# A two-layer diffusion backbone on one core: the pins of the norm seams, the order of the first loads, and the neighbourhood bias laid out by diagonals on the host

## The chip, the cores and the metric

The kernel runs as one program on one core of one Trainium2 chip. The metric is the device time of one execution in microseconds (us), as the median of several runs. Engines are named as in the profile: PE is TensorE (PEld its weight loads), DVE is VectorE, ACT is ScalarE, POOL is GpSimd, SP is SyncE, from whose queue nearly all transfers are issued.

## The reference, cut to what matters

Two streams of 256 tokens, the latent x and the context z, go through two layers of width 1024. With `mx` and `mz` the nine shift, scale and gate vectors that a matrix `w_mod` gives for a layer:

```
for l in range(2):
    x = x + 0.5 * mx[2] * swiglu(modulate(rms_norm(x), mx[0], mx[1]), w1, w3, w2)       # ffn1, and z likewise
    hx = modulate(rms_norm(x), mx[3], mx[4]) @ w_in                                     # and hz likewise
    mix_x, mix_z = token_mixing(hx, hz, ...)   # Fourier | neighbourhood attention | gated linear attention | GQA
    x = x + mx[5] * (mix_x @ w_out)                                                     # and z, in layer 0 only
    x = x + 0.5 * mx[8] * swiglu(modulate(rms_norm(x), mx[6], mx[7]), v1, v3, v2)       # ffn2, z in layer 0 only
# neighbourhood attention of a latent token: a window of 4 rows by 16 columns, and all context tokens
s_win = q . k_window * scale + rpb[head, row offset + 7, column offset + 15]
s_ctx = q . k_ctx * scale
```

The table `na_rpb` has 15 x 31 values for each of 4 heads and 2 layers.

## The kernel before, in words

Every product of activations and weights is done as three matmuls of reduced precision: weights are split into `whi` and `wlo`, activations into `hh` and `hl`, and hi·hi, lo·hi and hi·lo are summed. The activations lie as eight tiles X[d] of 128 channels by 512 tokens; stream s=0 is the latent half of a tile, s=1 the context half.

Weights come in the order in which they are used. SP loads a piece to one of three buffers `raw`; `w_conv` turns it into `whi` on ACT (L248) and `wlo` on DVE (L251), four buffers of each. `w_fill` converts until `lead` pieces lie ready. The order of instructions on each engine is set by a scheduler when the program is built; `issue_after(i)` keeps an instruction behind i, `after_products(n, fn)` calls fn once n more triples of products have been written, and `high_priority` moves instructions ahead.

Between two of the four parts of a layer lies a *norm seam*. The last part's output is added to X[d] by DVE (L479 of the ffn), ACT squares it (L308), DVE adds the last square to `ss` (L311), PE sums `ss` over the channels (`pb`, L323, from `norm_stat`), DVE makes `ms` (L331), POOL the power `rs` (L333), PE spreads it over the partitions (`pb<-cst,rs`, L340, from `norm_bcast`), and `norm_apply` makes for each d `htmp` (DVE L360), `hh` (ACT L362) and `hl`: on DVE (L367) for even d, on ACT and POOL (L364, L365) for odd d. PE does stream 0 first and begins the next part's products on it while stream 1 goes through this chain. `LAGS` says how many triples of products PE puts ahead of `pb` and ahead of the spreading, for each stream; `AHEAD` how many weight conversions are put in after the norm of stream 0 and how far the lead reaches at the end of a part; `HLD` which `hl` a conversion's `wlo` is put behind.

In the mixing, `bias_load` (L855) brings the neighbourhood bias of a head into one slot (two rows) of `biases` as four strips of 64 partitions, each of 64 x 4 runs of 256 B; in layer 0 three slots serve four heads, so that head 3 is loaded when slot 0 has been read for the last time (L760). `bias_mask` (L867, POOL) subtracts it from the window's mask. `ke` (L658 to L661, POOL) and `pa` (L672, PE) are steps of the gated linear attention, `rs` of L540 the power of a per-head norm (`rms_tok`), `nt` (L544, DVE) its result.

At the start the first eight columns of modulations are made by 32 loads of `w_mod` (`wfirst`, L137) and `modps` matmuls (L144), four groups q of two channel tiles each, while the first weight pieces and X are loaded.

## Time and profile before

| | |
|---|---|
| median of 3 runs | 1748.44 us (1746.54 to 1750.69) |
| the profiled execution | 1751.36 us |
| its span, first to last instruction | 1749.6 us |
| mean granted clock of TensorE | 0.990 of full speed |
| busy: PE / PEld / DVE / ACT / POOL | 1696.8 / 1478.8 / 1104.0 / 667.2 / 215.7 us |
| PE idle over the span | 1749.6 - 1696.8 = 52.8 us |

The span is the profiled execution's work; the 1.8 us between it and that execution's time lie ahead of the first and behind the last instruction. A clock of 0.990 is a mean over the span: for short stretches it is half. Busy time of PE holds matmuls that run at the half clock, so what the clock costs does not show as idle time.

### The profile page before, as it was taken

Reading aid. Unit: us, or ns where it says so; the run is one execution under the profiler, and the core shown is the slowest. Engines: PE = TensorE matmul, PEld = TensorE weight load, DVE = VectorE, ACT = ScalarE, POOL = GpSimd, SP = SyncE. Lnnn points to the kernel's source line nnn. Section 1 sums busy time; section 2 is a strip of 40 time slices with the busy share of each in tenths; the row PEclk is TensorE's granted clock in tenths of the full one; section 3 lists DMA queues with packets and bytes.
Section 4 is the critical chain, followed back from the end, with each engine's and each line's share of the span. In section 5 each row is a group of like instructions: output and inputs, shape, how many; then the busy total and the mean of one; then the engine's idle time right before and its main releaser. Section 6 shows DMA issues by size and latency. Waiting matters only on the chain.

```text
span 1749.6 us, 28022 instructions
## 1 busy us (share of the span) xinstructions
PE 1696.8 (97%) x11174; PEld 1478.8 (85%) x11174; DVE 1104.0 (63%) x1834; ACT 667.2 (38%) x1124; POOL 215.7 (12%) x252
## 2 busy tenths in 40 slices
PE   6999999998989999999999999999999899989999
...
PEclk9999999999989999999999999999999999999999
...
GB/s 331 186 192 161 216 204 193 109 100 114 76 54 47 25 157 176 199 165 182 109 96 72 97 199 223 169 196 225 180 79 90 98 121 80 53 122 198 182 194 137
DMA packets 92274, 254.03 MB, mean 145 GB/s; under 512 B 17648, under 2 KB 28144, under 8 KB 91760
## 3 DMA queue, kind: packets, MB, share of 16 engines
...
HBM read 251.16 MB, written 1.05 MB: 144 GB/s over the span
## 4 chain that ended last, share of the span: by engine, by line
PE 87%; DVE 4%; DMA 3%; ACT 2%; issue 1%; POOL 1%; SPq 1%; POOLq 0%; ACTq 0%
PE p L284 48%; PE py L284 23%; PE pt L284 6%; PE pyo L284 3%; DVE wlo L251 1%; DMA biases<-in_na_rpb_dram 1%; PE po L788 1%; PE prT L779 1%; PE sc L756 1%; ACT whi L248 1%; PE pf L284 1%; PE pa L672 1%; SPq L860 0%; DMA raw<-in_f1w_dram 0%; DMA wfirst<-in_wmodf_dram 0%
## 5 line engine op out<-in xcount | busy, mean ns | idle before, releaser
L248 ACT CAST whi<-raw 128x1024 fp32r<-128x1024 f32 (+2 forms) x356 | 339.3, 955 | 858.2 <-PE p L284 277.8
L251 DVE TENSOR_TENSOR wlo<-raw,whi 128x1024 fp32r<-128x1024 f32 (+2 forms) x356 | 397.8, 1120 | 219.3 <-ACT whi L248 212.4
L284 PE MATMUL p<-hl,whi 128*128 128x512 f32 (+1 forms) x1504 | 525.5, 351 | 2.0 <-DVE hl L367 1.4
L284 PE MATMUL p<-hh,wlo 128*128 128x512 f32 (+1 forms) x1504 | 525.2, 350 | 0.3 <-DVE wlo L251 0.3
L284 PE MATMUL p<-hh,whi 128*128 128x512 f32 (+1 forms) x1504 | 523.0, 351 | 1.8 <-ACT hh L362 1.1
L284 PEld LDWEIGHTS p<-hl,whi 128*128 128x128 f32 x1504 | 283.4, 189 | 40.5 <-DVE hl L367 1.9
L284 PEld LDWEIGHTS p<-hh,wlo 128*128 128x128 f32 x1504 | 283.3, 189 | 38.5 <-DVE wlo L251 0.6
L284 PEld LDWEIGHTS p<-hh,whi 128*128 128x128 f32 x1504 | 281.5, 189 | 40.5 <-ACT hh L362 2.0
L169 DVE CUSTOM_DVE_ANT_0 mprod<-wmod,crow 128x1024 f32<-128x1024 f32 x256 | 302.2, 1221 | 0.0
L284 PE MATMUL py<-gh,wlo 128*128 128x512 f32 (+1 forms) x764 | 265.0, 347 | 0.0
L284 PE MATMUL py<-gl,whi 128*128 128x512 f32 (+1 forms) x764 | 264.8, 347 | 0.0
L284 PE MATMUL py<-gh,whi 128*128 128x512 f32 (+1 forms) x764 | 264.3, 348 | 0.0
L311 POOL TENSOR_TENSOR ss<-ss,sq 128x512 f32<-128x512 f32 (+1 forms) x34 | 40.9, 1202 | 1045.4 <-ACT sq L308 1044.0
L409 DVE TENSOR_TENSOR g<-p,sl 128x512 f32<-128x512 f32 (+1 forms) x88 | 55.0, 625 | 179.4 <-PE p L284 178.9
L284 PEld LDWEIGHTS py<-gl,whi 128*128 128x128 f32 x764 | 143.9, 188 | 18.4
L284 PEld LDWEIGHTS py<-gh,wlo 128*128 128x128 f32 x764 | 143.8, 188 | 18.3
L284 PEld LDWEIGHTS py<-gh,whi 128*128 128x128 f32 x764 | 143.6, 188 | 18.2
L284 PE MATMUL pt<-whi,hl 128*128 128x256 f32 x448 | 133.0, 297 | 7.3 <-POOL hl L365 7.2
L284 PE MATMUL pt<-whi,hh 128*128 128x256 f32 x448 | 133.4, 298 | 1.5 <-ACT nt L533 1.3
L284 PE MATMUL pt<-wlo,hh 128*128 128x256 f32 x448 | 131.1, 293 | 0.0
L479 DVE SCALAR_TENSOR_TENSOR X<-py,mod,X 128x256 f32<-128x256 f32 x112 | 50.3, 481 | 96.5 <-PE py L284 96.4
L284 PEld LDWEIGHTS pt<-whi,hl 128*128 128x128 f32 x448 | 89.0, 199 | 9.7 <-POOL hl L365 9.2
...
## 6 DMA issues: line engine op xcount, KB each, us to landing
wmod<-in_wmodt_dram SPq DMA_DIRECT2D x128, 512.0 KB, 3.9
...
raw<-in_f1w_dram SPq DMA_DIRECT2D x32, 320.0 KB, 2.9
raw<-in_f2w_dram SPq DMA_DIRECT2D x32, 320.0 KB, 2.9
...
```

What stands on the lines that cost most here:

```text
L169: nc.vector.tensor_tensor_reduce(out=prod, in0=raw, in1=crow[:, s], scale=1.0, scalar=0.0, op0=ALU.mult, op1=ALU.add, accum_out=acc[:, s, ...
L248: nc.scalar.copy(hi[:, :k * n], raw[:, :k * n])
L251: wlo[0] = nc.vector.tensor_tensor(out=lo[:, :k * n], in0=raw[:, :k * n], in1=hi[:, :k * n].bitcast(F32), op=ALU.subtract).ins
L284: nc.tensor.matmul(ps, w, x, start=first and i == 0, stop=last and i == len(parts) - 1)
L311: (nc.vector if d == KD - 1 else eng).tensor_tensor(out=st["ss"][:, c], in0=st["ss"][:, c], in1=sq[:, c], op=ALU.add)
L409: nc.vector.tensor_tensor(out=g[:, :n], in0=p3[:, :n], in1=sl[:, :n], op=ALU.mult)
L479: nc.vector.scalar_tensor_tensor(out=X[mt][:, c], in0=py[:, c], scalar=mcol(l, m, mt, s), in1=X[mt][:, c], op0=ALU.mult, op1=ALU.add)
L672: nc.tensor.matmul(pa[w * b:w * b + w, c * w:c * w + w], ke[hs, k0:k0 + w], qe[hs, q0:q0 + w], start=True, stop=True)
L756: nc.tensor.matmul(ps[:, :n], q[:, e, (t % 2) * P:(t % 2 + 1) * P], ks[e][:, T - n:T], start=i == 0, stop=i == 1)
L779: nc.tensor.transpose(pt[:, c * P:(c + 1) * P], pr[e][:, (2 * half + i) * P:(2 * half + i + 1) * P], ident)
L788: last_mm = nc.tensor.matmul(po[64 * e:64 * e + 64, c0:c0 + P], vs[e][4 - nkt + kt], prT[:, (2 * e + i) * P:(2 * e + i + 1) * P], start=kt ...
```

## The change

1. Pins of the seams. `LAGS` for stream 1 goes from 6 to 12 triples (into the mixing) and 14 (into an ffn). A conversion put in at a seam has both its halves, `whi` and `wlo`, put behind the end of a stream's `norm_apply` (`st["end", s]`); before, `wlo` alone was put behind one `hl`. An ffn's first pieces are filled to three more behind the end of stream 0. The last square and addition of a norm get high priority.
2. `mm3` does hi·hi, lo·hi (`wlo`), hi·lo (`hl`), with the last two swapped.
3. First loads. All of X goes first, then a weight piece, the eight `wfirst` of group 0, a weight piece, the eight of group 1, two weight pieces, the last sixteen. `w_mod`'s first part is laid out on the host so that each `wfirst` is one run of 2 KB a partition (before: two of 1 KB).
4. Bias. The host lays `na_rpb` out by diagonals (`nab`), so that a load is one contiguous piece a partition: 768 KB for slots 0 to 2 in layer 0 and 256 KB for head 3, 1 MB in layer 1. The load stands behind the queries' unit; clearing and masking stand behind the last `rms_tok` power so far.

```diff
-LAGS = {3: ((6, 6), (4, 4)), 6: ((6, 6), (4, 4)), 0: ((6, 6), (4, 4))}
+LAGS = {3: ((6, 12), (4, 4)), 6: ((6, 14), (4, 4)), 0: ((6, 14), (4, 4))}
-AHEAD = {3: (1, 1), 6: (0, 2), 0: (0, 2)}
+AHEAD = {3: (1, 2), 6: (0, 2), 0: (0, 2)}
-HLD = (2, 6)
+HLD = (6, 6)
...
-            v = a["wmodf"][k * P:(k + 1) * P, 256 * q:256 * q + 256]
-            nc.sync.dma_start(out=raw.rearrange("p (m c) -> p m c", m=2),
-                              in_=bass.AP(tensor=v.tensor, offset=v.offset, ap=[list(v.ap[0]), [D, 2], list(v.ap[1])]))
+            nc.sync.dma_start(out=raw, in_=a["wmodf"][q, k])
...
-        nc.scalar.copy(hi[:, :k * n], raw[:, :k * n])
+        with tc.issue_after(after[0]) if after is not None else nullcontext():
+            nc.scalar.copy(hi[:, :k * n], raw[:, :k * n])
         lo = tp.tile([P, 1024], F32R, tag="wlo", name="wlo", bufs=nb)
-        with tc.issue_after(after) if after is not None else nullcontext():
+        with tc.issue_after(after[1]) if after is not None else nullcontext():
...
-        product(((wh[:, k, :], xh), (wh[:, k, :], xl), (wl[:, k, :], xh)), ps, first, last)
+        product(((wh[:, k, :], xh), (wl[:, k, :], xh), (wh[:, k, :], xl)), ps, first, last)
...
+        if d1 == KD:
+            st["end", s] = (last, st["hl", s, KD - 2][1])
...
                 for i in range(AHEAD[m][0] if n > S else 0):
-                    w_conv(after=st["hl", 0, HLD[0]])
+                    w_conv(after=st["end", 0])
             elif AHEAD[m][0]:
-                w_fill(after=st["hl", 1, HLD[1]])
+                w_fill(after=st["end", 1])
...
+                if ("end", 0) in st and start is None:
+                    lead[0] = LEAD + 1
+                    w_fill(after=st["end", 0])
+                    lead[0] = LEAD
...
-        def bias_load(heads):
-            rp = a["na_rpb"]
-            for hd in heads:
-                for r in range(4):
-                    o = rp.offset + ((l * 4 + hd) * 15 + 7 - r) * 31 - 48
-                    nc.sync.dma_start(
-                        out=biases[(r % 2) * 64:(r % 2) * 64 + 64, 2 * (hd % slots) + r // 2].rearrange("p (a b) -> p a b", a=4),
-                        in_=bass.AP(tensor=rp.tensor, offset=o, ap=[[1, 64], [31, 4], [1, 64]]))
+        def bias_load(h0, h1):
+            i = h0 % slots
+            nc.sync.dma_start(out=biases[:, 2 * i:2 * (i + h1 - h0)], in_=a["nab"][l][:, 2 * h0:2 * h1])
...
         def bias_ready():
-            nc.gpsimd.memset(biases[:, 2 * slots], 0.0)
-            bias_mask(range(slots))
+            with tc.issue_after(pw[0]):
+                nc.gpsimd.memset(biases[:, 2 * slots], 0.0)
+                bias_mask(range(slots))
...
-                        bias_load((3,))
+                        bias_load(3, 4)
...
-            "G": (gla_in,), "R": (gla_r,), "N": (bias_in, lambda: na_qk(nqT, pairs_q, V_NAQ), lambda: na_qk(nkS, pairs_all, V_NAK), na_v, bias_ready),
+            "G": (gla_in,), "R": (gla_r,), "N": (lambda: na_qk(nqT, pairs_q, V_NAQ), bias_in, lambda: na_qk(nkS, pairs_all, V_NAK), na_v, bias_ready),
...
                 for d in range(KD):
-                    if d % 2 == 0:
-                        load_x(d)
-                        load_x(d + 1)
-                        next(ld)
-                        mods_product(ps0, d // 2, first[0][-1])
+                    load_x(d)
                     norm_square(st, npool, d, 0, 2, nc.vector)
+                w_conv()
...
+def _diagonals(rpb):
+    import numpy as np
+
+    p = np.arange(P)[:, None, None]
+    key = np.arange(256)[None, None, :]
+    at = (7 - 2 * np.arange(2)[None, :, None] - p // 64 + key // 64) * 31 + p % 64 + key % 64 - 48
+    flat = rpb.reshape(-1)
+    head = 15 * 31 * np.arange(8)[:, None, None, None]
+    return flat[np.clip(head + at, 0, flat.size - 1)].reshape(2, 4, P, 2, 256).transpose(0, 2, 1, 3, 4).reshape(2, P, 8, 256)
```

How the instructions then stand is shown at three places. The first is the seam of layer 0 from ffn1 into the mixing. On DVE before, where stream 0's `htmp` and `hl` are being made (X_89 is the last tile of stream 1 to be added; what stands in brackets are the engines and queues whose semaphores the instruction waits for):

```order
L360 SCALAR_TENSOR_TENSOR htmp<-X_86,mod_97,pb 128x256 [waits DVE_49]
L367 SCALAR_TENSOR_TENSOR hl_3256<-htmp,mod_97,hh_3255 128x256 [waits Activation_49]
L479 SCALAR_TENSOR_TENSOR X_89<-py,mod_97,X_89 128x256 [waits PE_49]
L251 TENSOR_TENSOR wlo<-raw,whi 128x1024 [waits DMAHW4_49]
L251 TENSOR_TENSOR wlo<-raw,whi 128x1024 [waits DMAHW5_49]
L360 SCALAR_TENSOR_TENSOR htmp<-X_87,mod_97,pb 128x256 [waits DVE_49]
L360 SCALAR_TENSOR_TENSOR htmp<-X_88,mod_97,pb 128x256 [waits Pool_49]
L367 SCALAR_TENSOR_TENSOR hl_3269<-htmp,mod_97,hh_3268 128x256 [waits Activation_49]
L311 TENSOR_TENSOR ss<-ss,sq 128x256 [waits Activation_49]
```

On DVE after the change, at the same place:

```order
L485 SCALAR_TENSOR_TENSOR X_89<-py,mod_97,X_89 128x256 [waits PE_49]
L360 SCALAR_TENSOR_TENSOR htmp<-X_86,mod_97,pb 128x256 [waits Pool_49]
L360 SCALAR_TENSOR_TENSOR htmp<-X_87,mod_97,pb 128x256 [waits DVE_49]
L360 SCALAR_TENSOR_TENSOR htmp<-X_88,mod_97,pb 128x256 [waits DVE_49]
L360 SCALAR_TENSOR_TENSOR htmp<-X_89,mod_97,pb 128x256 [waits Pool_49]
L311 TENSOR_TENSOR ss<-ss,sq 128x256 [waits Activation_49]
L367 SCALAR_TENSOR_TENSOR hl_3273<-htmp,mod_97,hh_3272 128x256 [waits Activation_49]
L367 SCALAR_TENSOR_TENSOR hl_3286<-htmp,mod_97,hh_3285 128x256 [waits Activation_49]
L331 TENSOR_SCALAR ms<-pb 128x2 [waits PE_49]
L250 TENSOR_TENSOR wlo<-raw,whi 128x1024 [waits DMAHW5_49,Activation_49]
```

Two `wlo` stood between the last addition to X (L479, now L485) and the addition to `ss` (L311); now none does: one stands three rows ahead of that addition to X (not shown), the next behind `ms` (the last row shown). On POOL at the same seam, before (hl_3249 to hl_3288 are stream tiles of the odd d, the first four of stream 0, the last four of stream 1; DMAHW are the transfer lanes waited for):

```order
L365 TENSOR_TENSOR hl_3275<-htmp,hh_3274 128x256 [waits Activation_49]
L333 TENSOR_TENSOR rs<-ms,mhalf 128x2 [waits DVE_49]
L365 TENSOR_TENSOR hl_3288<-htmp,hh_3287 128x256 [waits Activation_49]
L867 TENSOR_TENSOR biases<-cst,biases 128x512 [waits DMAHW4_49,DMAHW6_49,DMAHW2_49,DMAHW1_49]
L867 TENSOR_TENSOR biases<-cst,biases 128x512 [waits DMAHW2_49,DMAHW7_49,DMAHW1_49,DMAHW0_49]
L365 TENSOR_TENSOR hl_3249<-htmp,hh_3248 128x256 [waits Activation_49]
L365 TENSOR_TENSOR hl_3262<-htmp,hh_3261 128x256 [waits Activation_49]
L867 TENSOR_TENSOR biases<-cst,biases 128x512 [waits DMAHW5_49,DMAHW6_49,DMAHW4_49,DMAHW3_49]
L365 TENSOR_TENSOR hl_3275<-htmp,hh_3274 128x256 [waits Activation_49]
L365 TENSOR_TENSOR hl_3288<-htmp,hh_3287 128x256 [waits Activation_49]
```

On POOL after the change:

```order
L365 TENSOR_TENSOR hl_3279<-htmp,hh_3278 128x256 [waits PE_49,Activation_49]
L365 TENSOR_TENSOR hl_3292<-htmp,hh_3291 128x256 [waits PE_49,Activation_49]
L333 TENSOR_TENSOR rs<-ms,mhalf 128x2 [waits DVE_49]
L365 TENSOR_TENSOR hl_3253<-htmp,hh_3252 128x256 [waits Activation_49]
L365 TENSOR_TENSOR hl_3266<-htmp,hh_3265 128x256 [waits Activation_49]
L365 TENSOR_TENSOR hl_3279<-htmp,hh_3278 128x256 [waits Activation_49]
L365 TENSOR_TENSOR hl_3292<-htmp,hh_3291 128x256 [waits Activation_49]
L606 TENSOR_TENSOR ku<-ku,kg 128x128 [waits DMAHW3_49,DMAHW4_49,DMAHW2_49,DMAHW5_49,DMAHW1_49,DMAHW6_49,DMAHW0_49,DMAHW7_49,DVE_49,Activation_49]
```

The three masks that stood among the `hl` of stream 1 are gone from the seam. The second place is head 3's bias in layer 0; POOL before:

```order
L658 TENSOR_TENSOR ke<-Bf 128x64x4 [waits PE_49]
L659 TENSOR_TENSOR ke<-Bb 128x64x4
L867 TENSOR_TENSOR biases<-cst,biases 128x512 [waits DMAHW4_49,DMAHW3_49,DMAHW7_49,DMAHW0_49,DVE_49]
L661 TENSOR_TENSOR ke<-ke,kg 128x512 [waits Activation_49]
L540 TENSOR_TENSOR rs_5007<-ms_5004,mhalf 128x4 [waits DVE_49]
```

POOL after the change:

```order
L666 TENSOR_TENSOR ke<-Bf 128x32x8 [waits PE_49]
L667 TENSOR_TENSOR ke<-Bb 128x32x8
L924 TENSOR_TENSOR go<-nt,row 128x512 [waits DVE_49]
L669 TENSOR_TENSOR ke<-ke,kg 128x512 [waits Activation_49]
L870 TENSOR_TENSOR biases<-cst,biases 128x512 [waits DMAHW2_49,DVE_49]
L548 TENSOR_TENSOR rs_4996<-ms_4993,mhalf 128x4 [waits DVE_49]
```

`ke` (L661, now L669) stood behind the mask (L867, now L870) and its four lanes; now the mask stands behind `ke` and waits for one lane, with the power `rs` still behind it. The third place is the masking in the mixing of layer 1; POOL before, in the stretch of the first `ke` steps:

```order
L658 TENSOR_TENSOR ke<-Bf 128x2x64 [waits PE_49,Pool_49]
L659 TENSOR_TENSOR ke<-Bb 128x2x64
L658 TENSOR_TENSOR ke<-Bf 128x4x32 [waits PE_49]
L659 TENSOR_TENSOR ke<-Bb 128x4x32
L540 TENSOR_TENSOR rs_12937<-ms_12934,mhalf 128x8 [waits DVE_49]
L661 TENSOR_TENSOR ke<-ke,kg 128x256 [waits Activation_49] x2
```

POOL after the change:

```order
L666 TENSOR_TENSOR ke<-Bf 128x2x64 [waits PE_49,Pool_49]
L667 TENSOR_TENSOR ke<-Bb 128x2x64
L548 TENSOR_TENSOR rs_12908<-ms_12905,mhalf 128x8 [waits DVE_49]
L878 MEMSET biases 128x256
L870 TENSOR_TENSOR biases<-cst,biases 128x512 [waits DMAHW5_49]
L870 TENSOR_TENSOR biases<-cst,biases 128x512 x3
L666 TENSOR_TENSOR ke<-Bf 128x4x32 [waits PE_49]
L667 TENSOR_TENSOR ke<-Bb 128x4x32
L669 TENSOR_TENSOR ke<-ke,kg 128x256 [waits Activation_49] x2
```

Clearing and four masks now stand between the power `rs` and the next `ke` steps; before they stood in the seam.

## Rows read from the trace of the kernel before

**Rows 1.** The page, the span in 40 equal slices: the busy tenths of PE, and the clock granted to TensorE in tenths.

```profile
PE   6999999998989999999999999999999899989999
PEclk9999999999989999999999999999999999999999
```

**Rows 2.** What PE waited for, by line: microseconds in total, times, longest.

```profile
PE pb L323 <- DVE ss L311: 8.8, 5, 2.2
PE pt L284 <- POOL hl L365: 7.2, 6, 3.0
```

**Rows 3.** Busy time by stretch: stretch, length, busy time (and instructions) of PE, PEld, DVE, ACT and POOL, granted clock, DMA share, GB/s. The first four are stretches at the half clock; the last is one of the mixing of layer 0.

```profile
400.80:404.20 3.40, 3.40 (x17) 3.40 (x17) 0.95 (x3) 0.84 (x2) 1.84 (x3) 0.50 0.83 197
414.50:417.90 3.40, 3.36 (x16) 3.36 (x16) 3.40 (x5) 2.42 (x4) 2.83 (x3) 0.51 0.03 8
513.40:523.70 10.30, 9.04 (x108) 8.42 (x109) 8.82 (x20) 2.47 (x6) 4.33 (x7) 0.50 0.20 52
1380.40:1387.30 6.90, 5.72 (x27) 5.72 (x28) 3.97 (x11) 3.28 (x8) 2.13 (x3) 0.51 0.75 182
...
540.00:598.00 58.00, 55.15 (x454) 47.23 (x453) 43.50 (x95) 36.65 (x103) 16.41 (x23) 1.00 0.13 38
```

**Rows 4.** Timeline of PE in the seam of layer 0 into the mixing: start, duration, what ran, and in brackets the idle time before it and what ended that.

```profile
397.65 0.38 PE L284 MATMUL pt<-whi,hl 128*128 128x256 f32 x1 [0.76 <-POOL hl L365]
400.25 0.61 PE L323 MATMUL pb<-ones,ss 128*128 128x1 f32 x4 [2.22 <-DVE ss L311]
...
413.85 0.39 PE L284 MATMUL pt<-whi,hl 128*128 128x256 f32 x1 [3.01 <-POOL hl L365]
```

**Rows 5.** Timeline of DVE in the same seam.

```profile
394.91 0.48 DVE L479 SCALAR_TENSOR_TENSOR X<-py,mod,X 128x256 f32<-128x256 f32 x1
395.31 3.37 DVE L251 TENSOR_TENSOR wlo<-raw,whi 128x1024 fp32r<-128x1024 f32 x2
...
399.78 0.41 DVE L311 TENSOR_TENSOR ss<-ss,sq 128x256 f32<-128x256 f32 x1
...
414.23 0.54 DVE L367 SCALAR_TENSOR_TENSOR hl<-htmp,mod,hh 128x256 fp32r<-128x256 f32 x1
...
415.08 1.55 DVE L367 SCALAR_TENSOR_TENSOR hl<-htmp,mod,hh 128x256 fp32r<-128x256 f32 x1
```

**Rows 6.** Timeline of POOL in the same seam.

```profile
411.86 1.26 POOL L867 TENSOR_TENSOR biases<-cst,biases 128x512 f32<-128x512 f32 x1 [2.83 <-DMA biases<-in_na_rpb_dram]
413.07 1.42 POOL L365 TENSOR_TENSOR hl<-htmp,hh 128x256 fp32r<-128x256 f32 x2
415.07 1.28 POOL L867 TENSOR_TENSOR biases<-cst,biases 128x512 f32<-128x512 f32 x1 [0.58 <-DMA biases<-in_na_rpb_dram]
```

**Rows 7.** Head 3's bias in layer 0: timelines of DVE (the last reading of slot 0 ahead of the load), POOL, PE and DVE again.

```profile
504.98 0.68 DVE L760 CUSTOM_DVE_ANT_1 pr<-sc,biases 128x512 f32<-128x512 f32 x1
...
510.10 1.26 POOL L867 TENSOR_TENSOR biases<-cst,biases 128x512 f32<-128x512 f32 x1 [3.75 <-DMA biases<-in_na_rpb_dram]
...
512.63 0.75 PE L672 MATMUL pa<-qe,ke 32*32 32x32 f32 x64 [2.24 <-POOL ke L661]
514.66 1.97 PE L788 MATMUL po<-prTs,nv 128*64 128x128 f32 x16 [1.27 <-DVE prTs L782]
...
513.58 0.42 DVE L544 TENSOR_TENSOR nt<-nt,rs 128x256 f32<-128x256 f32 x1 [4.88 <-POOL rs L540]
```

**Rows 8.** Transfers: the strips issued between 401 and 409 us; from the page, one kind of weight piece over the whole run. Columns: count, KB each, us from issue to landing.

```profile
biases<-in_na_rpb_dram SPq DMA_DIRECT2D x9, 64.0 KB, 7.2
...
raw<-in_f1w_dram SPq DMA_DIRECT2D x32, 320.0 KB, 2.9
```

**Rows 9.** Timelines of PE in the seams of layer 0 from the mixing into ffn2 and of ffn2 into layer 1's ffn1, and one row of DVE in the first of them.

```profile
647.07 0.39 PE L284 MATMUL p<-hl,whi 128*128 128x256 f32 x1 [1.38 <-DVE hl L367]
650.82 0.60 PE L323 MATMUL pb<-ones,ss 128*128 128x1 f32 x4 [1.09 <-DVE ss L311]
...
1016.15 0.61 PE L323 MATMUL pb<-ones,ss 128*128 128x1 f32 x4 [1.71 <-DVE ss L311]
...
648.51 1.21 DVE L251 TENSOR_TENSOR wlo<-raw,whi 128x1024 fp32r<-128x1024 f32 x1
```

**Rows 10.** Timeline of PE in the seam of layer 1 into the mixing, the pieces with idle time ahead of them, the longest.

```profile
1378.98 0.38 PE L284 MATMUL pt<-whi,hl 128*128 128x256 f32 x1 [0.76 <-POOL hl L365]
1381.58 1.01 PE L323 MATMUL pb<-ones,ss 128*128 128x1 f32 x4 [2.22 <-DVE ss L311]
1395.05 0.39 PE L284 MATMUL pt<-whi,hl 128*128 128x256 f32 x1 [1.86 <-POOL hl L365]
...
1403.11 0.39 PE L284 MATMUL pt<-whi,hl 128*128 128x256 f32 x1 [0.46 <-POOL hl L365]
```

**Rows 11.** Timeline of POOL in the mixing of layer 1, around the place where the masks now stand.

```profile
1443.77 1.80 POOL L540 TENSOR_TENSOR rs<-ms,mhalf 128x8 f32<-128x8 f32 x1 [1.93 <-DVE ms L538]
1445.54 1.87 POOL L661 TENSOR_TENSOR ke<-ke,kg 128x256 f32<-128x256 f32 x2
```

**Rows 12.** The start: a piece of the chain that ended last, PE's last waiting there, and the rate of all transfers from 23 to 30 us.

```profile
20.89 7.52 DMA raw<-in_f1w_dram
...
30.80 0.38 PE L284 MATMUL p<-hh,wlo 128*128 128x256 f32 x1 [0.29 <-DVE wlo L251]
...
DMA packets 1870, 2.59 MB, mean 370 GB/s; under 512 B 126, under 2 KB 1613, under 8 KB 1869
```

35 lines of the change are left out of this document (19 added, 16 removed).

## The prediction

> **What bounds the kernel now.** I read the slices of the page first: PE stands at nine tenths or more in all but a few slices, and the slices that fall short lie at the seams and in the two mixings; the granted clock dips at the first mixing [rows 1]. So a change is worth only what it takes from PE's idle time (52.8 us over the span, by the table) or from the half clock. The waits by line come next: of PE's idle time in the middle of the run, the largest entries are `pb` waiting for the sum `ss` on DVE and `pt` waiting for POOL's `hl` [rows 2], which are both places in a norm seam. The stretches by clock are third: in four of them TensorE was granted half speed, 1.2 instead of 2.4 GHz, and in each of these stretches the busy time is spent at double length [rows 3]. Each began right at or just after an idle time of PE of 2.2 us or more: 2.22 us before 400.25, 3.01 us before 413.85 [rows 4], 2.24 us before 512.63 [rows 7], 2.22 us before 1381.58 [rows 10]. Idle times of 1.09 to 1.86 us [rows 9, 10] had none behind them. So a long stall here costs its length, and half of PE's busy time in the slow stretch after it.
>
> **The seam of layer 0 into the mixing.** DVE is the engine to look at. It added the last tile of X at 394.91, then did two `wlo` that took 3.37 us, and came to `ss` at 399.78 [rows 5]; PE waited 2.22 us for it [rows 4]. In the new order no `wlo` stands between, and PE has 36 matmuls ahead of `pb` in place of 18. At half clock 17 matmuls took 3.40 us [rows 3], 0.20 each, so at full clock they take 0.10 or a little more, and 36 are some 4 us of cover. From the last X at 394.91 to the end of `ss` were 5.3 us [rows 5]; without the two `wlo` they are 1.9. This stall goes. The second is POOL's: a mask waited 2.83 us for its strips, with `hl` at 413.07 queued behind it [rows 6], and PE waited 3.01 us for that `hl` [rows 4]. No mask stands in the seam now, and no strips either. I take away 0.76 + 2.22 + 3.01 = 5.99 us of idle time and half of 3.40 + 3.36 us of busy time [rows 3], 3.4 us; I leave 0.9 us, since DVE now does a `wlo` (1.2 us, [rows 9]) and the gate weights' halves between `ms` and stream 1's first `htmp`, and PE reaches stream 1 after 36 + 12 + 24 matmuls or so. **-8.5 us**; bounds -9.4 (nothing left) and -6.0 (one stall of 3 us with no slow stretch, or the clock as it is).
>
> **The strips and the pieces.** Nine strips of 64 KB took 7.2 us each from issue to landing; a 320 KB weight piece landed in 2.9 us [rows 8]. For a piece of 768 KB or 1 MB I estimate from the latter at most 2.9 x 1024 / 320 = 9.3 us. In the new order it is issued with the attention's units, and its masks stand behind the last per-head power, many steps later, so it is off the path. The weight pieces on SP that stood behind nine or more strips come sooner; no PE wait names them, so I count nothing.
>
> **Head 3's bias in layer 0.** After slot 0's last reading at 504.98 the strips were there only at 510.10; `ke` and the power behind the mask were late, PE waited 2.24 and 1.27 us, and DVE 4.88 us for `rs` [rows 7]. A slow stretch of 9.04 us of busy time follows [rows 3]. `ke` now stands ahead of the mask, so the 2.24 us go. Behind the mask `rs` remains. One transfer of 256 KB lands in 2.9 us or less [rows 8], at 505.66 + 2.9 = 508.6 in place of 510.1, and the step from there to `nt`, 3.48 us, loses the `ke` in it: `nt` starts 1.5 us earlier by the landing alone, and 2.4 to 3.4 with the `ke` (1.87 us for two, [rows 11]) gone. I leave 1.0 us of the 3.51, and take the slow stretch as gone, since no idle of 2.2 us is left: 2.5 + 9.04 / 2 = **-7.0 us**. Bounds: -8.0 (all idle gone), and -1.5 (the clock falls all the same, as some short idle times together might do, and 2 us of stall stay).
>
> **The ffn seams of layer 0 and into layer 1.** Here nothing slows, but PE stood 1.38 + 1.09 and then 1.71 us [rows 9]; one `wlo` of 1.2 us lay ahead of `ss` in each. They go behind the apply, and 42 matmuls lie ahead of `pb`. What is late next is the second weight group, whose conversion now begins only behind the end of a stream's apply: an ACT and a DVE piece, 1.0 and 1.2 us. I count 1.0 and 0.5 us as left: **-1.5** and **-1.2 us**, bounds -2.0 to -0.4 each. The last seam, with stream 0 only, keeps its order, and is left at nothing.
>
> **The seam of layer 1 into the mixing** is the first one over again: 0.76 + 2.22 + 1.86 + 0.46 = 5.30 us idle [rows 10], half of 5.72 us [rows 3], 0.6 us left: **-7.6 us**, bounds -8.5 and -5.0.
>
> **The masks' new place.** Masks and clearing were in the seams and are now between a power and the next `ke`. In layer 1 that is 4 x 1.3 us and the clearing, some 5.5 us of POOL [rows 6], behind `rs` at 1443.77 and ahead of `ke` [rows 11]. In the new order PE has more matmuls of `pt` ahead of the `pa` that needs it, which hides the delay if they are enough: 0 to 5.5 us, of which I take half, **+2.8 us**. In layer 0 there are three masks, and POOL's `ke` is not waited for at that place now: nothing. A mask also slows DVE: `hl` took 1.55 us beside the mask at 415.07, and 0.54 just before it [rows 5, 6]. The Trainium skill's page "SBUF — State Buffer" (section Who interferes with whom) has a rule for this: a DVE instruction with two SBUF inputs contends with a GpSimd instruction that reads SBUF. By that rule every mask in the mixing holds up a `wlo` or `hl` beside it; in these rows the trace agrees. By the sum, where DVE had free time (43.50 us busy of 58, [rows 3]), it costs nothing; by the rule at its worst, the first rival. The rest of the mixing comes in a new order; by the 2.85 us that PE stood in those 58 us I give that 0, +-3 us.
>
> **The start.** PE was last held there by the `whi`, `wlo` of a weight piece that landed 28.4 us after the start, two pieces behind the eight `wfirst` [rows 12]. Now one weight piece is behind X and the second behind group 0: 0.5 MB fewer ahead of the first product, at 370 GB/s [rows 12] 1.4 us. PE had no wait after 30.80, so it is passed on: **-1.3 us**, bounds 0 (the last `wfirst` decides) and -2.5. The run of 2 KB is given nothing: packets under 2 KB were 1613 of 1870 in that stretch, and the rate 370 GB/s all the same.
>
> **The swap in `mm3`** costs the same three matmuls; `wlo` must be there one matmul earlier, `hl` one later, 0.1 us: nothing.
>
> **Sum.** -1.3 - 8.5 - 7.0 - 1.5 - 1.2 - 7.6 + 2.8 = -24.3 us. Against the profiled execution, 1751.36, that is 1727.1; the median lies 2.9 us under it, and 1748.44 - 24.3 = **1724.1 us**. All bounds together reach from -35 to -5 us.
>
> **Rivals.** *The mixing takes some back through the masks*: they delay `ke` in full (+5.5 for +2.8), and each of the seven costs DVE 1.55 - 0.54 = 1.0 us on the path. For it speaks the `hl` of [rows 5]; against it, that DVE is not full there. -24.3 + 2.7 + 7.0 = -14.6: 1734 us. Chance 0.17. *Head 3's stretch stays slow* (-1.5 for -7.0), since short idle times are left together there and the mask is still waited for: -18.8, 1730 us. Chance 0.13. *The seams wait for weights instead*: conversions pinned behind the apply are late for the second group, and 2.5 us stay in each mixing seam, with the slow stretch: -3.5 and -3.2 for -8.5 and -7.6, nothing from the ffn seams. For it speaks that `wlo` alone takes 1.2 us and stands in one queue with stream 1's `htmp`; against it, that pieces converted ahead lie ready, as `p` hardly waits for `wlo` now [rows 12]. -24.3 + 5.0 + 4.4 + 2.7 = -12.2: 1736 us. Chance 0.1. *Slower*: the same pins at worst. If all four pieces of an ffn's first two groups are converted only behind the apply, PE stands for four times 1.2 us less what it has to do, in each of five seams; with the slow stretches that follow it decides from some 6 us a seam, +28 us against the sum, and at 7 us a seam gives 1748.4 - 24.3 + 35 = 1759 us. For it speaks that both halves are pinned now, against it that PE has two streams' products of the pieces converted before. Chance 0.05. *No change to measure*: all terms at their poor ends, 1748.4 - 4.8 = 1744 us, or a little worse, 0.04.
>
> **Numbers.** The forecast holds with 0.51, between 1714 and 1729. The range to 1738 takes in the first three rivals (0.40 together), and 1714 most of the good ends: 0.09 and the tail of the good ends are left out. What a measurement can tell from no change is 0.2%, 3.5 us: faster 0.91, same 0.04, slower 0.05.
>
> **What would show it.** In the profile after: `pb` on `ss` nearly gone from PE's waits; no `biases` mask between `hl` in the seams; no half clock at the two seams into the mixing, nor behind head 3's load; `ke` of layer 1 late by no more than 3 us; `p` on `wlo` or `whi` under 1.5 us a seam. A slow stretch at any of the three places, worth 3 to 5 us each, or a new wait of PE on conversions would make the prediction wrong.

## The result, and the profile after

The changed kernel takes 1732.60 us (median; 1725.29 to 1733.49) against 1748.48 us for the kernel before in the same runs. The ratio is 0.9899 with an interval of 0.9877 to 0.9921, so some 16 to 18 us less: faster, inside the range of 1714 to 1738, but 8.5 us short of the 1724.1 that was forecast. The profiled execution has a span of 1731.6 us against 1749.6, 18.0 us less; the sums below go by that pair. Line numbers are those of the new file: L250 is `wlo`, L485 the addition to X, L669 `ke`, L870 the mask, L924 `go`.

The slices of the page, as in [rows 1]:

```profile
PE   6999999999999999999999999999999998989999
PEclk9999999999999999999999999999999999999999
```

Each digit is a slice of some 43 us. Both dips of the first mixing are gone from PE's line, and the one in the clock's line too; so is the dip where the second mixing begins. One is now in the second half of the second mixing (1429 to 1472 us), and that of the last seam is left. PE's waits by line, the answer to [rows 2]:

```profile
PE pb L323 <- DVE ss L311: 12.5, 1, 12.5
PE prT L787 <- ACT pr L771: 2.0, 1, 2.0
PE ptr L750 <- POOL go L924: 1.8, 1, 1.8
PE p L283 <- DVE wlo L250: 1.1, 2, 0.7
PE pa L680 <- POOL ke L669: 0.7, 1, 0.7
```

`pb` on `ss` is now the one wait at the very start (all of X comes before the first `modps`); the four in the seams are gone, and so is `pt` on POOL's `hl`. Among the new ones are the waits for `pr`, for `go` and, small, for `wlo` in the ffn seams and for `ke` in layer 1.

Now the mixings, of the kernel before (the seam for layer 0 alone) and of the changed one. Columns as in [rows 3]; the rows of 26 us are the seam at the mixing's beginning, the long ones the whole mixing up to `pyo`, the first matmul of its output product.

```profile
394.69:420.69 26.00, 19.93 (x132) 18.99 (x131) 16.95 (x28) 11.58 (x26) 10.97 (x13) 0.87 0.53 100
394.69:597.77 203.08, 188.99 (x2185) 171.43 (x2183) 147.93 (x299) 116.90 (x268) 86.15 (x98) 0.96 0.27 68
1376.02:1523.08 147.06, 135.56 (x1364) 119.41 (x1363) 109.66 (x232) 85.54 (x190) 58.90 (x74) 0.95 0.36 93
```

```profile
392.92:418.92 26.00, 25.10 (x179) 22.99 (x178) 17.97 (x33) 14.72 (x28) 7.53 (x9) 1.00 0.48 151
392.92:585.69 192.77, 185.19 (x2184) 166.12 (x2183) 143.55 (x300) 116.58 (x267) 89.08 (x98) 0.99 0.23 71
1362.19:1388.19 26.00, 25.35 (x177) 22.33 (x176) 18.58 (x34) 15.70 (x30) 6.62 (x9) 1.00 0.59 189
1362.19:1504.11 141.92, 132.97 (x1364) 118.39 (x1363) 105.40 (x233) 85.78 (x189) 57.54 (x74) 0.96 0.31 96
```

In the seam of layer 0 PE did 179 instructions in 26 us where it did 132, at full clock where it had 0.87 on the mean. But the two mixings as wholes gained only 10.3 and 5.1 us. The seam as the DVE timeline shows it, the answer to [rows 5]:

```profile
394.27 0.47 DVE L485 SCALAR_TENSOR_TENSOR X<-py,mod,X 128x256 f32<-128x256 f32 x1
394.67 1.64 DVE L360 SCALAR_TENSOR_TENSOR htmp<-X,mod,pb 128x256 f32<-128x256 f32 x4
396.23 0.42 DVE L311 TENSOR_TENSOR ss<-ss,sq 128x256 f32<-128x256 f32 x1
...
398.97 0.16 DVE L331 TENSOR_SCALAR ms<-pb 128x2 f32<-128x2 f32 x1 [1.53 <-PE pb L323]
```

From the last X to the end of `ss` it is 2.4 us (5.3 before), and DVE now waits for PE's `pb`, not PE for `ss`. At head 3's bias in layer 0, the timelines of POOL and PE (the answer to [rows 7]):

```profile
493.53 1.72 POOL L924 TENSOR_TENSOR go<-nt,row 128x512 f32<-128x512 f32 x1
495.21 1.28 POOL L669 TENSOR_TENSOR ke<-ke,kg 128x512 f32<-128x512 f32 x1
498.00 1.27 POOL L870 TENSOR_TENSOR biases<-cst,biases 128x512 f32<-128x512 f32 x1 [1.51 <-DVE ATd L685]
...
495.30 0.44 PE L750 MATMUL ptr<-cst,go 128*128 128x128 f32 x2 [1.81 <-POOL go L924]
```

The mask no longer waits for a transfer, and PE has no wait of 0.3 us or more in the 35 us behind it; but PE now stands 1.81 us in front of it, for the GQA's `go`. In the mixing of layer 1 the masks, and a wait near its end (POOL; then ACT and PE):

```profile
1422.17 6.40 POOL L870 TENSOR_TENSOR biases<-cst,biases 128x512 f32<-128x512 f32 x4
...
1474.35 1.28 ACT L1030 ACT_TABLE_LOAD   x1
1475.65 0.60 ACT L1030 ACTIVATE mix<-pt 128x512 f32<-128x512 f32 x1
1476.14 1.04 ACT L247 CAST whi<-raw 128x1024 fp32r<-128x1024 f32 x1
1477.20 1.28 ACT L771 ACT_TABLE_LOAD   x1
...
1479.36 0.80 PE L787 MATMUL prT<-cst,pr 128*128 128x128 f32 x4 [2.05 <-ACT pr L771]
```

The gate's SiLU (L1030) has come between two exponentials of a softmax, with a table load before and after it and a weight cast in between; PE waits for the second exponential.

To place gains inside the mixings, whose instructions come in another order now, I counted the projection matmuls (`pt`, `pf`, `pg`) on PE's timeline. The table has the time from the mixing's first matmul, in us:

| | 100th | 300th | 400th | 600th | 800th | end |
|---|---|---|---|---|---|---|
| layer 0, before | 22.2 | 55.3 | 71.4 | 102.6 | 163.7 | 203.1 |
| layer 0, after | 14.8 | 46.9 | 62.7 | 97.2 | 153.3 | 192.8 |
| difference | -7.4 | -8.4 | -8.8 | -5.4 | -10.4 | -10.3 |
| layer 1, before | 21.0 | 52.7 | 68.0 | 118.8 | | 147.1 |
| layer 1, after | 14.6 | 44.1 | 59.9 | 108.1 | | 141.9 |
| difference | -6.4 | -8.6 | -8.1 | -10.7 | | -5.1 |

So by the 300th matmul both seams have paid what they pay. Behind that, layer 0 adds only 1.9 us, and layer 1 gives 3.5 back: it is 10.7 us ahead at the 600th matmul and loses 5.6 in the last 34 us.

### The profile page after: what moved, and what is told of

It reads as the page before. It is cut to its first block, busy times and chain, and to the rows that moved or that the text cites. A ratio compares the mean times of both kernels' runs of the same rounds, so it can differ in the third digit from the quotient of the medians.

```text
span 1731.6 us, 27978 instructions
## 1 busy us (share of the span) xinstructions
PE 1690.0 (98%) x11174; PEld 1473.6 (85%) x11174; DVE 1097.7 (63%) x1834; ACT 664.3 (38%) x1124; POOL 218.9 (13%) x252
## 4 chain that ended last, share of the span: by engine, by line
PE 86%; DVE 6%; POOL 2%; ACT 2%; issue 2%; DMA 2%; SPq 0%; ACTq 0%; POOLq 0%; DVEq 0%
PE p L283 48%; PE py L283 24%; PE pt L283 5%; PE pyo L283 3%; DVE wlo L250 1%; DMA wfirst<-in_wmodf_dram 1%; PE po L796 1%; PE prT L787 1%; PE pf L283 1%; POOL rs L548 1%; PE sc L764 1%; ACT whi L247 1%; DVE htmp L360 0%; DVE nt L552 0%; PE pa L680 0%
## 5 line engine op out<-in xcount | busy, mean ns | idle before, releaser
L250 DVE TENSOR_TENSOR wlo<-raw,whi 128x1024 fp32r<-128x1024 f32 (+2 forms) x356 | 396.5, 1116 | 266.5 <-ACT whi L247 264.3
L311 POOL TENSOR_TENSOR ss<-ss,sq 128x512 f32<-128x512 f32 (+1 forms) x34 | 40.4, 1190 | 1041.6 <-ACT sq L308 1041.4
L409 ACT ACTIVATE sl<-p 128x512 f32<-128x512 f32 (+1 forms) x88 | 48.0, 546 | 262.9 <-PE p L283 262.9
L283 PE MATMUL pt<-whi,hh 128*128 128x256 f32 x448 | 131.7, 294 | 0.6 <-ACT gv L956 0.3
L485 DVE SCALAR_TENSOR_TENSOR X<-py,mod,X 128x256 f32<-128x256 f32 x112 | 50.3, 480 | 86.9 <-PE py L283 86.7
```

What stands on the lines that cost most here:

```text
L250: wlo[0] = nc.vector.tensor_tensor(out=lo[:, :k * n], in0=raw[:, :k * n], in1=hi[:, :k * n].bitcast(F32), op=ALU.subtract).ins
L283: nc.tensor.matmul(ps, w, x, start=first and i == 0, stop=last and i == len(parts) - 1)
L311: (nc.vector if d == KD - 1 else eng).tensor_tensor(out=st["ss"][:, c], in0=st["ss"][:, c], in1=sq[:, c], op=ALU.add)
L409: nc.scalar.activation(sl[:, :n], p1[:, :n], AF.Silu)
L485: nc.vector.scalar_tensor_tensor(out=X[mt][:, c], in0=py[:, c], scalar=mcol(l, m, mt, s), in1=X[mt][:, c], op0=ALU.mult, op1=ALU.add)
```

## The experiments

The kernel before ran beside each of them, with medians from 1750.6 to 1753.2 us; kernels that did not run side by side are therefore compared by their ratios to it.

**The three parts alone.** From the kernel before, the hunks of the diff that belong to the pins, to the bias and to the first loads, each by itself (named here, not printed; the swap in `mm3` is in none of them):

```
 e1_pins:   LAGS, AHEAD, HLD, st["end", s], w_conv(after=...), the ffn's w_fill, the last square's priority
 e2_bias:   _diagonals, bias_load(h0, h1), order of "N", issue_after(pw[0])
 e3_start:  order of load_x, w_conv and mods_load; wmodf laid out by groups
```

> The pins of the seams alone (LAGS, AHEAD, both halves of a conversion behind the end of the apply, the ffn's fill, the last square ahead); bias strips, first loads and the order in mm3 as before. If the terms add up (theory): the waits for ss in the two mixing seams go with the slow stretch behind each, 2.2 + 1.7 and 2.2 + 2.9 us, and 2.7 us in the ffn seams, -10 to -13 us, and the wait for POOL's hl behind the masks stays. If the strips set the end of the mixing seams (rival): PE reaches stream 1 earlier and waits there for the masks by what it gained, since the strips land when they land: the wait of pt for POOL's hl grows by 2 to 4 us a seam, and only -3 to -6 us are left.

> The bias alone (diagonals from the host, one piece a layer behind the queries, masks behind a per-head power); pins, first loads and mm3 as before. If the terms add up: the wait for POOL's hl goes from both mixing seams (-3.0 - 1.7 and -2.7 us), head 3 gives -7.0, the masks cost +2.8: -11 to -12 us. If head 3's place stays slow, as the profile of the whole change has it (a stall of 1.8 us on POOL's go, and half clock behind it): -5 to -7 us, with the half clock again between 490 and 525 us.

> The first loads alone (all of X first, weight pieces between the groups of wfirst, 2 KB runs). My term: -1.3 us, between 0 and -2.5, and the first py of the first ffn begins 1.3 to 1.8 us earlier than in the kernel before (164.79 us there). Rival: the last wfirst decides and nothing is left: within 0.3 us of before.

Measured: the pins 0.9960 (0.9946 to 0.9973), 5.8 us by the medians; the bias 0.9927 (0.9913 to 0.9942), 12.9 us; the start 0.9990 (0.9981 to 1.0000), 1.3 us. By these ratios the three add up to 1.23%, and the whole is 1.01%; the intervals are too wide to make anything of the difference. The first expectation's theory fell, and its rival holds in size and in what it names, the strips, though the wait grew at another step than `hl`. Timelines of POOL and PE in the seam of layer 0 with the pins alone:

```profile
404.39 1.26 POOL L875 TENSOR_TENSOR biases<-cst,biases 128x512 f32<-128x512 f32 x1 [5.91 <-DMA biases<-in_na_rpb_dram]
...
406.38 0.69 PE L342 MATMUL pb<-cst,rs 128*128 128x128 f32 x2 [6.18 <-POOL rs L335]
```

The wait for `ss` is gone, but the power `rs`, the next step of the same chain, now stands behind a mask that waits 5.91 us for its strips, and PE stands 6.18 us for it. So the pins alone earn nothing in the mixing seams: the 300th matmul comes at 56.1 and 52.3 us, against 55.3 and 52.7 before. The two ffn seams are 1.4 and 0.9 us shorter; the worth of the pins at the mixing seams needs the bias out of the way. The bias alone gave what the sum says of it, though not by the terms of the sum. Its mixing seams are 4.4 and 6.1 us shorter by the 300th matmul, with a wait of 1.7 us for an `hl`, one of 0.5 for `ss` and some half clock left in each. The rest of the mixing of layer 0 is 3.3 us shorter, where 7.0 was forecast, and that of layer 1 is 1.5 shorter, where 2.8 longer was forecast. Its profile has the wait for `go` of 1.8 us too, and the half clock behind it (500.4 to 503.8 us). The start is as forecast: the first `py` began at 162.56 us, in place of 164.79. Single profiles scatter here: the five with the old order of loads have it between 163.3 and 165.7 us, the nine with the new one between 162.2 and 164.1, and the means are 1.5 us apart.

**The masks taken out.** In the changed kernel the eight subtractions of L870 are left out.

```diff
         def bias_mask(heads):
             for hd in heads:
                 b = biases[:, 2 * (hd % slots):2 * (hd % slots) + 2]
-                nc.gpsimd.tensor_tensor(out=b, in0=bmid(cst[:, C_NM:C_NM + 256], 2), in1=b, op=ALU.subtract)
+                pass
```

> The whole change without the masks' subtraction on POOL (all eight L870 instructions left out, so the attention's bias is used as loaded; everything else is computed). It prices the masks' new place. My term: they cost 2.8 us, so -2 to -4 us against the whole change. If they hold up the mixing (rival, each costs POOL's queue and DVE): -7 us or more, to 1725 us or less, and the half clock near 496 and near 1452 us goes. If the mixing's stalls have other causes: within 1 us of the whole change, and the half clock stays.

Measured: 0.9909 (0.9894 to 0.9924), which is no faster than the whole change at 0.9899 and 0.9898. In the profile the first 300 matmuls take what they took, layer 1's mixing is 4.1 us shorter (137.8) and layer 0's 6.5 us longer (199.3, with the half clock at 494 to 501 and 535 to 542 us), in an order that is again another. None of the three expectations came as written: the half clock near 496 stayed, but the total did not fall. So the masks' place does not show as what the gain was lost to, and the first rival of the prediction finds no support here; a price of the masks alone this run does not give, since it changed the order of both mixings.

**The whole change again**, unchanged.

> The whole change once more, unchanged, with a second profile. Its four runs were 1725.29 and three from 1732.53 to 1733.49. If the half clock comes and goes between executions of one program (theory), the runs spread over 5 to 10 us again and this profile has its half-clock stretches at other places or of other lengths than the first (there: near 496, 1452, 1462, 1479 and 1537 to 1547), while PE's waits are the same to 0.3 us. If the program sets them (rival), the same places and lengths come back and the runs agree within 3 us but for one.

Measured: 0.9898 (0.9877 to 0.9918), 1732.45 us, five of six runs within 1.3 us and the sixth 4 us above. Most of PE's larger waits came back to 0.1 us, that for `go` with 1.80 us among them; that for `ss` at the start is 0.7 us shorter, and in the mixings three smaller ones (for `ATd`, `nm` and `nt`) are 0.6 to 0.7 longer. The half clock did not come back as it was: none in layer 0's mixing. The first row is a stretch of the first profile of the changed kernel, the second the whole mixing of layer 0 in this one:

```profile
496.40:500.20 3.80, 3.80 (x82) 3.24 (x82) 1.32 (x6) 2.21 (x8) 2.29 (x3) 0.55 0.17 50
```

```profile
392.12:584.43 192.31, 183.86 (x2184) 164.92 (x2183) 143.89 (x300) 116.47 (x267) 88.96 (x98) 1.00 0.23 72
```

The first had 3.8 us of busy time at 0.55, which by the reckoning of the prediction costs 1.7 us; the mixing without it is only 0.46 us shorter, since PE's idle time there is 8.45 us in place of 7.58. Taken instruction by instruction, PE fell 1.3 us behind in the slow stretch, and half of that came back 10 us later, where the second profile waits 0.69 us for the operands of a `po` (at 508.97) and the first, being late, does not. Both theories were half right: the place changes from execution to execution, the total hardly does.

**Head 3's piece alone.** The kernel before, with only the second load of layer 0 in the new form; POOL's order there is that of the kernel before.

```diff
                     if hp == 0 and p == 0 and slots < 4:
-                        bias_load((3,))
+                        nc.sync.dma_start(out=biases[:, 0:2], in_=a["nab"][l][:, 6:8])
                         bias_mask((3,))
```

> The kernel before with one thing changed: head 3's second load in layer 0 comes as one piece of 256 KB from the diagonals in place of four strips; the order on POOL in layer 0 is the one of the kernel before, with ke behind the mask. It prices the term that came out short (head 3's place, -7.0). If stall and slow stretch there are worth what I took: the piece lands 1.5 us or more earlier, pa's wait of 2.24 us falls under 1 us, the half clock behind it (513 to 524 us) goes, -4 to -7 us on the mixing of layer 0. If the half clock is cheap there (rival: PE has short waits anyway, and matmuls of 32 columns do not take twice as long): -1 to -3 us, with or without half clock in the records.

Measured: 0.9986 (0.9972 to 1.0000), 2.6 us by the medians. Timelines of POOL and of PE (all of PE's idle times of 0.3 us and more from 495 to 525 us):

```profile
508.97 1.80 POOL L867 TENSOR_TENSOR biases<-cst,biases 128x512 f32<-128x512 f32 x1 [1.67 <-DVE rsum L769]
510.74 1.29 POOL L661 TENSOR_TENSOR ke<-ke,kg 128x512 f32<-128x512 f32 x1
...
503.02 0.66 PE L788 MATMUL po<-prTs,nv 128*64 128x128 f32 x8 [1.02 <-DVE prTs L782]
505.46 0.58 PE L756 MATMUL sc<-nkS,qhi 128*128 128x256 f32 x1 [0.49 <-DVE nm L760]
```

The mask no longer waits for a transfer, and the waits of 2.24 and 1.27 us of [rows 7] are gone, even with `ke` still behind the mask. The half clock is there all the same, from 504.8 to 511.6 us, after idle times of 1.02 and 0.49 us. By the runs the rival of this expectation holds. The one profile lies at the theory's edge: its mixing of layer 0 takes 199.0 us against 203.1, and of these 4.1 us 3.3 are idle time. Where they came from can be read from the two timelines. `pa` began 118.0 us after the mixing's first matmul with the piece and 117.9 with the strips: what the stall had cost there, the slow stretch, now ahead of `pa`, cost instead. The gain came behind `pa`, where the kernel before had its wait of 1.27 us and its own slow stretch. With the stalls taken out, the same instructions took some 3.6 us longer in the old slow stretch, and some 2.7 us longer in the new one (estimates from their times in both profiles). So of the 4.5 us some 0.9 was earned. The stall itself may not be worth all it looks: `ke` was done 1.4 us earlier than before (116.5 us after the first matmul in place of 117.9), and PE at the speed of the kernel before would have come at 115.7 and have waited some 0.8 us.

In the kernel with the start alone the strips were as late as ever, 4.3 to 4.9 us from issue to landing (a timeline of POOL, and the longer of PE's two idle times of 0.3 us and more from 495 to 515 us):

```profile
508.34 1.28 POOL L865 TENSOR_TENSOR biases<-cst,biases 128x512 f32<-128x512 f32 x1 [3.79 <-DVE qe L652]
...
500.27 0.66 PE L786 MATMUL po<-prTs,nv 128*64 128x128 f32 x8 [1.01 <-DVE prTs L780]
```

POOL stood 3.79 us ahead of the mask, and PE did not wait for `ke` behind it at all. Two things differ: PE was at half clock from 501.8 to 508.6 us, ahead of the stall's place instead of behind it, and its order has 40 projection matmuls between the last `ptr` ahead of `pa` (at 504.9 us) and `pa`, where the kernel before has 26. Both bring it later to `pa`; this run does not part them. PE's 700th projection matmul of the mixing was at 131.7 us there with strips, at 131.5 us with the piece, and at 135.6 us in the profile on which the prediction was made.

**The form alone.** The kernel before with the bias in one piece a layer, its load and its masks where they were.

```diff
         def bias_in():
-            bias_load(range(slots))
+            bias_load(0, slots)
             yield
...
-                        bias_load((3,))
+                        bias_load(3, 4)
```

> The kernel before with the bias laid out by diagonals and loaded in one piece a layer, at its old place in the units and with no pin on the masks: the form alone. The masks then stand behind the second hl of stream 0 on POOL and wait for the piece. If it is the strips that cost (their many short runs), the waits in the mixing seams shrink by 2 to 4 us and head 3's place gains: -4 to -8 us against before. If it is the place of the masks ahead of the norm's hl and rs (theory): POOL is held by the piece's landing, 7 us or so, and 3.9 or 5.2 us of masks, now ahead of rs and six hl, so the seams get longer: +2 to +10 us at the seams, less what head 3 gains.

Measured: 0.9977 (0.9960 to 0.9994), 5 us by the medians. Timelines of POOL and PE in the seam of layer 0:

```profile
401.35 3.72 POOL L862 TENSOR_TENSOR biases<-cst,biases 128x512 f32<-128x512 f32 x3 [4.47 <-DMA biases<-in_nab_dram]
...
406.47 0.69 PE L340 MATMUL pb<-cst,rs 128*128 128x128 f32 x2 [3.16 <-POOL rs L333]
```

POOL waits 4.47 us for the piece and masks for 3.72, ahead of `rs` and `hl`, as the theory had it, and by the 300th matmul the seams are 1.0 and 1.7 us longer than before (56.3 and 54.4 us): one wait of 3.16 us on `rs` stands in the place of one of 3.01 on `hl` [rows 4]. What it gained lies behind the seam of layer 0 (144.7 us from the 300th matmul to the end, 147.8 before); the kernel with the start alone, which has the strips, took 144.3 there, so that is not shown to be the form's. So the form alone earns nothing in the seams; there it is the place of load and masks that earns.

**No swap, and `go` on DVE.** Two edits of the changed kernel, each alone and then together:

```diff
-        product(((wh[:, k, :], xh), (wl[:, k, :], xh), (wh[:, k, :], xl)), ps, first, last)
+        product(((wh[:, k, :], xh), (wh[:, k, :], xl), (wl[:, k, :], xh)), ps, first, last)
...
-                nc.gpsimd.tensor_tensor(out=o[:, :2 * w].rearrange("p (t n) -> p t n", t=2), in0=nv_, in1=gain, op=ALU.mult)
+                nc.vector.tensor_tensor(out=o[:, :2 * w].rearrange("p (t n) -> p t n", t=2), in0=nv_, in1=gain, op=ALU.mult)
```

> The whole change without the swap in mm3. My term: nothing, within 1 us of the whole change. Rival: since wlo is now converted behind the apply and is wanted one matmul earlier by the swap, undoing it gives 1 to 2 us back at the ffn seams (the waits of p for wlo of 0.70 and 0.38 us go, and waits for hl take their place); and since the three parts alone add to -20 us against -16 of the whole, the swap might cost up to 4 us by the order it gives the mixing.

> The whole change with the queries' and keys' gain (go, L924) multiplied on DVE instead of POOL. PE waits 1.81 us for it near head 3's place, and the half clock follows. DVE does such a product in 0.7 us where POOL took 1.7. If that stall and what it triggers is what was left of head 3's gain (theory): -3 to -5 us against the whole change (1.2 us of stall and 1.7 to 3.4 of half clock), no half clock between 490 and 505. If the mixing is full of such chains and the next one takes its place (rival): within 1.5 us, with another wait near by.

> The whole change without the swap in mm3 and with go on DVE, the two edits that gave something alone (1728.6 and 1726.3 against 1732.5 us). If they add: 1722 to 1723 us, -30 us against the kernel before. If each gave its part by the order that the mixing happened to get: 1725 to 1732 us.

Measured: without the swap 0.9876 (0.9856 to 0.9897), with `go` on DVE 0.9859 (0.9834 to 0.9884), both 0.9893 (0.9874 to 0.9912). In microseconds 1728.6, 1726.3 and 1731.2. Without the swap the stretch from the first `pyo` of layer 0 to ffn2's first `py` is 0.45 us shorter (181.59 against 182.04). The wait for `wlo` in it falls from 0.70 to 0.41 us, and a wait of `pyo` for X of 0.61 us goes as well; in the next ffn seam the wait for `wlo` of 0.38 us is gone, and the stretch is 0.1 us shorter. The intervals of the two totals overlap, so the rest of the 3.8 us is not told apart from nothing. With `go` on DVE the runs (1720.8 to 1730.5) lie all under those of the whole change beside it (1731.7 to 1736.7), and it is the fastest kernel here. But not by the stall that it was made for: PE still waits 1.4 us there, in place of 1.8, and the mixings are 189.3 and 137.6 us long in yet another order. Put together, the two edits give less than either. The expectation that they add fell.

The traces show a part of why. ACT in layer 1 with `go` on DVE, to be read beside the rows of ACT above:

```profile
1468.55 0.72 ACT L771 ACTIVATE pr<-pr,nm 128x512 f32<-128x512 f32 x1 [0.42 <-DVE nm L768]
...
1470.68 0.60 ACT L1030 ACTIVATE mix<-pt 128x512 f32<-128x512 f32 x1
```

Both exponentials now stand ahead of the SiLU, and PE's wait of 2.05 us for `pr` is gone. Without the swap it is the same, and layer 1's mixing takes 140.4 us. With both edits the SiLU is between the exponentials again, PE waits 2.04 us, and the mixing takes 143.3. So in layer 1 the difference goes with the order that each edit happened to bring. In layer 0 the two kernels with `go` on DVE agree, 189.3 and 188.5 us, against 192.3 to 193.3 in the three profiles without. The place of the SiLU is not enough by itself: with the masks left out it stands between the exponentials too, and PE has no wait there.

**The SiLU taken out.** In the changed kernel the gate's nonlinearity is left out, so that no table load comes between the exponentials (9 such loads are left in the whole run, of 15).

```diff
-                nc.scalar.activation(gr, rr[p], AF.Silu)
+                nc.scalar.activation(gr, rr[p], AF.Identity)
```

> The whole change with the gate's SiLU (L1030, ACT) replaced by a plain copy of its argument, so the gate's nonlinearity is left out. In layer 1 of the whole change this SiLU stands between two of the softmax's exponentials and brings two loads of ACT's function table, 1.28 us each, with a weight cast of 1.04 us between; PE waits 2.05 us for the exponential behind them, which it did not before. If that is what the end of layer 1's mixing lost (theory): the wait of prT for pr (2.0 us, once) goes, the mixing of layer 1 gets 2 to 5 us shorter (141.6 to 141.9 us now), and the run is 3 to 6 us faster than the whole change, since layer 0 loses table loads too. If PE has other waits ready behind it (rival): within 1.5 us of the whole change.

Measured: 0.9877 (0.9858 to 0.9896), 1728.2 us, some 4 us under the whole change; the four runs lie within 1.8 us. The wait of `prT` for `pr` of 2.0 us is gone and the mixing of layer 1 takes 138.3 us instead of 141.6 to 141.9:

```profile
1360.34:1498.62 138.28, 131.43 (x1364) 116.90 (x1363) 105.08 (x233) 83.29 (x187) 57.48 (x74) 0.98 0.32 99
```

That is 3.3 to 3.6 us, within the theory's 2 to 5. Up to the 600th projection matmul the mixing runs as in the first profile of the whole change, to 0.1 us (108.0), and the last stretch takes 30.3 us in place of 33.9; the second profile has 109.2 and 32.4. The intervals of the two totals overlap, so the total alone would not show it. A whole kernel built on it, with SiLU from the softmax's own table and `go` on DVE:

```diff
...
-                nc.scalar.activation(gr, rr[p], AF.Silu)
+                nc.scalar.activation(gr, rr[p], AF.Exp, scale=-1.0)
+                nc.vector.tensor_scalar(out=gr, in0=gr, scalar1=1.0, scalar2=None, op0=ALU.add)
+                nc.vector.reciprocal(gr, gr)
+                nc.vector.tensor_tensor(out=gr, in0=rr[p], in1=gr, op=ALU.mult)
```

> A whole kernel again: the whole change with go on DVE, and SiLU made as x / (1 + exp(-x)) with the table that the softmax uses, three more DVE instructions a tile. If table loads and go are both on the path: 1720 to 1724 us. If the order that the mixing gets decides, as with the pair of edits run before: 1725 to 1732 us.

Measured: 0.9896 (0.9880 to 0.9912), 1731.8 us. Layer 1's mixing is short (138.4), layer 0's long (196.2): a wait of `pt` for `nm` on DVE of 2.8 us is new there. The rival holds: the order that the mixing happens to get takes back what the edit gives.

## Why the prediction came out as it did

By the stages of the two profiles, in us:

| term | forecast | measured | from |
|---|---|---|---|
| start | -1.3 | -1.8 | first `py` 164.79 to 163.02 |
| seam of layer 0 into the mixing | -8.5 | -8.4 | 300th matmul |
| head 3, and the rest of that mixing | -7.0 | -1.9 | 300th matmul to the end |
| the two ffn seams | -1.5, -1.2 | -1.0, -0.8 | `pyo` to `py`, 183.02 to 182.06; `py` to `py`, 365.33 to 364.54 |
| seam of layer 1 into the mixing | -7.6 | -8.6 | 300th matmul |
| masks in layer 1, and the rest of that mixing | +2.8 | +3.5 | 300th matmul to the end |
| last seam's ffn, first half | 0 | +1.0 | first `p` to first `py`, 69.71 to 70.75 |
| sum | -24.3 | -18.0 | spans |

**The seams are right, and for the reasons given.** The waits for `ss` and for the `hl` behind the masks are gone, no half clock is left there, and 0.65 to 0.90 us of idle time stays in 26 us. The pins alone add one thing that the sum did not say: at the mixing seams the two parts depend on each other, since `rs` stood behind the masks as well as `hl`.

**The step that failed is head 3's: "2.5 + 9.04 / 2".** The whole stretch behind the 300th matmul gained 1.9 us, where this term alone had 7.0. Columns as in [rows 3], for the kernel before and for the second profile of the changed one:

```profile
450.00:597.77 147.77, 139.75 (x1861) 126.31 (x1858) 113.19 (x243) 85.81 (x209) 69.56 (x78) 0.97 0.20 53
439.05:584.43 145.38, 138.06 (x1864) 123.42 (x1863) 113.99 (x245) 86.48 (x212) 75.03 (x83) 1.00 0.18 53
```

The stall is gone in the second row and there is no half clock at all, and yet it is only 2.4 us shorter: 1.7 us of busy time, and 0.7 us of idle time (8.02 and 7.32 us). So most of the idle time that was taken away came back at other places, 1.80 us of it for `go`. And what the half clock would give back was put too high, for three reasons.

First, the slow stretch was taken as gone because no idle time of 2.2 us was left. The kernel before itself speaks against that: besides the four stretches of [rows 3] it had two more between its first and last microsecond, which the prediction does not name.

```profile
1482.80:1489.70 6.90, 6.34 (x59) 4.50 (x59) 6.00 (x19) 4.28 (x12) 3.59 (x6) 0.51 0.20 75
1557.90:1561.30 3.40, 3.37 (x16) 3.08 (x16) 3.40 (x9) 3.37 (x10) 1.47 (x2) 0.50 0.18 71
```

The one began after waits of 0.33 and 0.60 us, the other after 1.04 and 1.12. And with the piece alone the half clock came back after waits of 1.02 and 0.49 us; in the two profiles of the changed kernel it is there once and missing once. Second, half of the busy time is more than it cost here: some 3.6 us in place of 4.5 in the kernel before, and 1.3 in place of 1.7 in the first profile of the changed one. (Of the 3.6 only 1.7 show as shorter busy time in the rows above; what takes the rest in the new order is not shown.) Third, a PE that is late by the half clock finds less to wait for, which gave half of those 1.3 us back and put the piece's `pa` where the strips' had been. Stall and slow stretch were read from one execution as two costs that add, and in part they stand for each other. In the seams, where matmul follows matmul, the sums with the same price came out within 0.1 and 1.0 us.

The rival *head 3's stretch stays slow*, at 1730 us, is nearest in time to the 1732.6 measured, but it is not what happened: the mask was not waited for any more, and the second profile has the same time with no slow stretch there. That the time lies in the range is owed to its upper part, which was drawn for the rivals; the sum is 8.5 us off, and some 5 of them are in this one term.

**The masks' term came near its size for another reason.** The masks ran from 1422.17 us, just behind the 400th matmul; PE's wait for `ke` behind them, at 1431.0, is 0.68 us, and at the 600th matmul the mixing was further ahead of the old one than at the 300th. So at most 0.7 of the 2.8 us is seen. What took 5.6 us in the last 34 us of that mixing is ACT's order, in part: 2.05 us of PE's wait for an exponential behind two table loads and a cast, and half clock around it. Leaving out the SiLU gave 3.3 to 3.6 us of that back. That the mixing would come in a new order was in the sum as 0, +-3; this is where its plus went, and no view of the kernel before could show it, though the order of ACT's instructions could have.

**Whether the last seam's +1.0 us is the change's is not shown.** Its waits of 1.04 us for `rs` and 1.11 for `hh` are those of before (1.04 and 1.12). From layer 1's first `pyo` to the last ffn's first `py` the two profiles of the changed kernel took 105.2 and 105.7 us, the kernel before 104.2; they have 6.8 us of half clock in it, the kernel before 3.4. Over all profiles here the nine kernels with the pins took 104.7 to 105.7 us and the five without 104.1 to 105.0. The prediction had this seam at nothing because its order stays. It does not quite: of the conversions ahead of the norm's `ms`, two now stand behind the apply; no wait of PE names them.

**The start and the ffn seams** came within 0.5 us; the second weight group's `wlo` is what is late next there, 0.70 and 0.38 us, as said. The swap was put at nothing; undoing it took 0.3 and 0.4 us from these waits.

What stays open: the order of a mixing changes with every edit, and stages of 188 to 199 us in layer 0 and of 138 to 143 us in layer 1 go with orders that I could tie to one instruction only for the SiLU's place in layer 1. Of what `go` on DVE gave, some 4 us by the profiles lie in layer 1, where the SiLU moved, and some 3 in layer 0; which instruction gives those, with only 0.4 us less waiting at `go`, is not shown.
